# When the second half's operands are made, and on which engine the gate's minimum runs, in a hybrid decoder block

## The chip, the cores and the metric

The kernel runs on one core of a Trainium2 chip. Its engines are TensorE (PE in the profile, with its weight loads as PEld), VectorE (DVE), ScalarE (ACT) and GpSimd (POOL); SyncE (SP) issues the DMA transfers. Each engine runs its own queue strictly in order and waits on semaphores for the others. The metric is the time of one execution on the device in microseconds; the runs of the kernel before have a median of 2060.56 us.

## The reference

One decoder layer over 2048 positions of width 1024. The parts that matter here:

```python
h = rmsnorm(x, norm1_g[l])
proj = h @ w_in[l]
p_q, p_k, p_v, p_g, p_a, c_b, c_c, c_h = jnp.split(proj, splits, axis=-1)
gate_logits = (p_a @ w_gate_up[l] + b_gate[l]).astype(jnp.float32)
log_a = (jax.nn.log_sigmoid(gate_logits) / GATE_NORMALIZER)
o = gla_chunked(q, k, v, log_a)
o = rmsnorm(o, gla_norm_g[l])
o = o * jax.nn.silu(p_g)
u = c_c * c_h
o_conv = c_b * causal_depthwise_conv(u, conv_w[l])
x = x + jnp.concatenate([o_gla, o_conv], axis=-1) @ w_out[l]
h2 = rmsnorm(x, norm2_g[l])
x = x + (silu(h2 @ w_ffn_gate[l]) * (h2 @ w_ffn_up[l])) @ w_ffn_down[l]
return rmsnorm(x, norm_f_g)
```

## The kernel before

The 2048 positions are cut into four blocks of 512, and two blocks make a half. The input projection, then the output projection, then the feed-forward part run half by half. Everything is kept transposed: a tile has 128 features on the partitions and 512 positions.

**Products.** A float32 operand is split into a high and a low part of a shorter type (`split`, L162: a copy on ScalarE, L163, makes the high part, a subtraction on VectorE, L164, the low part). A product is then three matmuls: high x high, high x low, low x high (`product_step`, L443, lines 448 to 450). Over these, a Strassen scheme with seven products instead of eight combines four quarters of the weights with four quarters of the operands (`unit`, L452). The right-hand operands have seven kinds, B11, T1, T2, B21, T3, B22 and T4, each with four tiles; T1 to T4 are differences of quarters. The weights of a unit come as A11, S1, S2, A12, S3, S4, A22; they are split just ahead of their product into four buffers `wq`, so a split can be at most three products ahead. A product has 12 matmuls, a unit seven products. In a unit, c11 is copied out of the bank of the first product (`copied`, L476, copy on L480) before the third product S2 adds into the same bank; the later sums are made on VectorE (`plus`, L472, L473).

**The input projection** (`in_proj`, L749) has twelve units in each half: u = 0 to 3 make keys, queries and values, u = 4 and 5 the output gate (`silu`, L509, L512 on ScalarE), u = 6 to 11 the short convolution. The operands of the first half are made at the start (`build_first`). Those of the second half, x scaled by the norm's factors, are made in the background of the first half: `h1_ahead` (L646) calls `combine` (L278). That loads a quarter of x (`fetch`), scales it on VectorE (`quad`, `scaled`, L615), makes the differences on GpSimd and hands each operand to `put`. `put` stores three kinds whole (T3, B22 and T4, named in `WHOLE`) as float32. It splits the other four and stores high and low parts. Between the halves `load_pairs` (L662) loads them: a kind stored in two parts by one transfer, a kind stored whole by `load_whole`, which splits it after loading. An operand's tile can be loaded once the last product of the first half with its predecessor is done, since there are 28 operand tiles (`opp`).

**The gate.** `gate` (L691) multiplies the operands with the low-rank weights (32 matmuls into `a_ps`, L702), copies and splits the result (`a_sb`), and makes four products z (L724), each followed by `forget_gate` (L730). With s = z + b that computes log sigmoid(s) = min(s, 0) - ln(1 + exp(-|s|)): Abs, Exp and Ln on ScalarE (L733, L735, L736), the minimum and the subtraction on VectorE (L734, L737), then four scans over 128 positions and two small Exp on ScalarE (`em`, `el`).

**The recurrence.** `gla_half` (L801) goes over eight chunks of 128 positions in a half. Each chunk loads 14 small tiles, and has Exp, Ln and Square on ScalarE and small matmuls on TensorE.

**Order.** Background work is a list of generators. After each product `tick` (L241) counts `pace` and runs one step of the first generator at each second tick, or at each tick while `hurry` is set. The list of the first half holds the gate of the first half, row statistics, then `unhurried`, then `h1_ahead`; `gla_half(0)` is appended after the Silu units, and `gate(1)` when the second half begins. This sets the order in which the instructions are written. From it a scheduler fixes the order on each engine when the program is built, with its own estimate of when each instruction is ready. `tc.issue_after` (in `behind`, L155) asks that an instruction be queued after another one on the same engine; it adds no wait for another engine. The loads of ScalarE's function tables are put in afterwards, before each function that is not in the table set then resident.

Of the kernel before, what the change touches and what calls it, by code (L numbers as in the profile page):

```python
# [10 lines left out]
F32 = mybir.dt.float32  # L11
# [3 lines left out]
AF = mybir.ActivationFunctionType  # L15
ALU = mybir.AluOpType
# [3 lines left out]
P = 128  # L20
D = 1024
SEQ = 2048
PB = 512
# [21 lines left out]
WHOLE = ("T3", "B22", "T4")  # L45


C_G1, C_G2, C_GF, C_BG, C_GN, C_CW = 0, 8, 16, 24, 26, 27
N_SMALL = 39

# [2 lines left out]
def tile_hymba_block(ctx, tc, x, xt, win, wa, wgu, wout, wffn, wdown, wdown_first, small, out):  # L53
    nc = tc.nc
    act, dve, pool, pe = nc.scalar, nc.vector, nc.gpsimd, nc.tensor

    def pool_of(name, bufs, **kw):
        return ctx.enter_context(tc.tile_pool(name=name, bufs=bufs, **kw))

    const = pool_of("const", 1)  # L60
# [6 lines left out]
    dram = pool_of("dram", 1, space=DRAM)  # L67
# [19 lines left out]
    dve.memset(eps[:], EPS)  # L87
    sml = const.tile([P, N_SMALL], F32, name="sml")
    nc.sync.dma_start(sml[:], small)
    wgu_sb = mixer.tile([96, 256], F32R, name="wgu_sb")  # L90
    wa_sb = mixer.tile([P, 23 * 32], F32R, name="wa_sb")
    dve.memset(wa_sb[:].bitcast(F32), 0.0)
# [10 lines left out]
            [dram.tile([P, PB], F32, name=f"{name}{b}_{i}") for i in range(n)] for b in range(NB)  # L103
        ]

    def made_ahead(name, n):
        return dram.tile([P, PB] if n in WHOLE else [P, 2, PB], F32, name=name)

    s_kq, s_d, s_v, s_g = scratch("sk", 4), scratch("sd", 2), scratch("sv", 4), scratch("sg", 4)
    s_x1 = scratch("sx", KD)  # L110
# [15 lines left out]
        n: [made_ahead(f"sh{n}_{k}", n) for k in range(4)] for _, n in PRODUCTS  # L126
    }
    s_h1 = {
        n: [made_ahead(f"si{n}_{k}", n) for k in range(4)] for _, n in PRODUCTS
    }  # L130

    def col(c):
        return sml[:, c : c + 1]
# [7 lines left out]
    def bt(name, shape=(P, PB)):  # L141
        return bx[0].tile(list(shape), F32, name=name, tag="b")

    def load(dst, src):
        return nc.sync.dma_start(dst, src)

    def store(dst, src):
        return nc.sync.dma_start(dst, src)

    last_hi, last_lo, raw_loads = [], [], []  # L150
    last_out = []
    second_weights, unit_splits, unsplit = [], [], []

    @contextmanager
    def behind(marks):  # L155

        with ExitStack() as stack:
            for m in marks:
                stack.enter_context(tc.issue_after(m.ins))
            yield  # L160

    def split(src, hi, lo):  # L162
        last_hi[:] = [act.activation(hi, src, AF.Copy)]  # L163
        last_lo[:] = [dve.tensor_tensor(lo, src, hi.bitcast(F32), ALU.subtract)]  # L164
        return last_lo[0]
# [62 lines left out]


    background = []  # L230
    pace, ahead, hurry = [0], [], []

    def step():
        while background:
            try:
                next(background[0])
                return
            except StopIteration:
                background.pop(0)

    def tick():  # L241
        pace[0] += 1
        if pace[0] % 2 == 0 or hurry:
            step()
        elif ahead and pace[0] % 4 == 1:
            next(ahead[0], None)

# [8 lines left out]

    def unhurried():
        hurry.clear()
        yield

    def pause(n):
        for _ in range(n):
            yield
# [14 lines left out]
    def combine(src, g, rb, put):  # L278


        order = [kj for k in range(4) for kj in ((k, 0), (k, 1), (k + 4, 1), (k + 4, 0))]
        ahead = deque()

        def fetch():
            if order:
                k, j = order.pop(0)
                h = bt("h")
                load(h[:], src(k, j))
                ahead.append((k, j, h))

        def quad():
            k, j, h = ahead.popleft()
            fetch()
            return scaled(col(g + k), rb[j], h)

        fetch()
        fetch()
        for k in range(4):
            b11 = quad()
            put("B11", k, b11)  # L300
            yield
            b12, t1 = quad(), bt("t1")
            pool.tensor_tensor(t1[:], b12[:], b11[:], ALU.subtract)
            put("T1", k, t1)
            yield
            b22 = quad()
            pool.tensor_tensor(t1[:], b22[:], t1[:], ALU.subtract)
            put("T2", k, t1)
            yield
            pool.tensor_tensor(b12[:], b22[:], b12[:], ALU.subtract)  # L310
            put("T3", k, b12)
            yield
            b21 = quad()
            put("B21", k, b21)
            yield
            pool.tensor_tensor(t1[:], b21[:], t1[:], ALU.subtract)
            put("T4", k, t1)
            yield
            put("B22", k, b22)
            yield  # L320

    def build_first(quad, w):

# [128 lines left out]
    def unit(src, ops, into=None, onto=None, raw=None):  # L452

        w = unit_weights(src, raw)
        unit_splits[:] = last_hi + last_lo
        with behind(unit_splits):
            for y, o in unsplit:
                split(y[:], o[:, 0, :], o[:, 1, :])  # L460
        unsplit.clear()

        def mul(i, o=None):
            first = o is None
            o = bank() if first else o
            n, m = PRODUCTS[i]
            for k in range(len(ops[m])):
                product_step(o, w[n], ops[m], k, first)
            tick()
            return o  # L470

        def plus(t, o):  # L472
            dve.tensor_tensor(t[:], o[:], t[:], ALU.add)  # L473
            return t

        def copied(name, o, at):  # L476
            if onto is not None:
                return plus(onto[at], o)
            t = tt(name) if into is None else into[at]
            last_out[:] = [act.activation(t[:], o[:], AF.Copy)]  # L480
# [132 lines left out]
    def scaled(g, rb, h, into=None):  # L613
        y = h if into is None else into
        last_scaled[:] = [dve.scalar_tensor_tensor(y[:], h[:], g, rb[:], ALU.mult, ALU.mult)]  # L615
        return y
# [29 lines left out]
    def h1_ahead():  # L646

        def put(n, k, h):
            if n in WHOLE:
                store(s_h1[n][k][:], h[:])  # L650
                return
            hi, lo = [bx[0].tile([P, PB], F32R, name=e, tag="b") for e in ("hi", "lo")]
            split(h[:], hi[:], lo[:])
            for e, y in enumerate((hi, lo)):
                store(s_h1[n][k][:, e, :], y[:].bitcast(F32))

        for b in (2, 3):
            rbs[b] = rows_rstd(squares[b][:, :, 0], tables=False)
            yield
        yield from combine(lambda k, j: xt[2 + j, :, k, :], C_G1, (rbs[2], rbs[3]), put)  # L660

    def load_pairs(src):  # L662
        ops = no_operands()
        for _, n in PRODUCTS:
            ops[n] = [(load_whole if n in WHOLE else load_pair)(p) for p in src[n]]
        return ops

    def load_whole(src):
# [61 lines left out]
    def forget_gate(b, i, z, em, dn, el):  # L730
        bg = col(C_BG + i)
        t1, t2 = bt("g1"), bt("g2")
        act.activation(t1[:], z[:], AF.Abs, bias=bg)  # L733
        dve.tensor_scalar(t2[:], z[:], bg, 0.0, ALU.add, ALU.min)  # L734
        act.activation(t1[:], t1[:], AF.Exp, scale=-1.0)  # L735
        act.activation(t1[:], t1[:], AF.Ln, bias=one_t)  # L736
# [515 lines left out]
    for i in range(6):  # L1252
        load(carry[16 * i : 16 * i + 16, 0:2, :], wgu[0:16, :].rearrange("p (h c) -> p h c", c=P))
    ops, first, differences = build_h()
# [10 lines left out]
    ops = load_pairs(s_h1)  # L1265
# [122 lines left out]
```

## Time and profile before

| | |
|---|---|
| median of 3 runs | 2060.56 us (2059.81 to 2061.47) |
| span of the profiled execution | 2059.3 us |
| TensorE busy | 2018.4 us, 98% |
| VectorE, ScalarE, GpSimd busy | 1425.3, 959.7, 859.8 us |
| mean granted clock of TensorE | 0.996 |

In the profile's rows, a group is given by line, engine, operation, and output<-input by the program's names, with the count; then its busy time, the mean duration of one in ns, and the idle time of the engine before it. A row of waits reads "who <- for whom: us in total, times, longest". A row of the chain or of the timeline has start and duration in us. A row of windows has the length of the window and then pairs of busy time and count for PE, PEld, DVE, ACT and POOL, the granted clock, the share of DMA and GB/s. Matmuls overlap, so the time of one is read from the starts of two. SPq rows are the issues of DMA transfers.

### The profile page before, as it was taken

The numbers are of one execution on the slowest core, as the hardware profiler recorded it, in microseconds if no ns is written. First come the engines' busy times: TensorE is split into PE (matmuls) and PEld (weight loads), VectorE is DVE, ScalarE is ACT, GpSimd is POOL, SyncE is SP. The second block draws the span as 40 slices with busy tenths as digits, with TensorE's granted clock in tenths as the row PEclk, the third lists the DMA queues.
The fourth block names the chain that finished last, engine by engine and source line by source line (L and its number), as shares of the span: only waits on it lengthen the run. The fifth ranks groups of instructions, "written<-read, shape, count | busy, mean of one in ns | idle before, by whom it ended". The sixth has DMA issues, their size and how long they took to land.

```text
span 2059.3 us, 27063 instructions
## 1 busy us (share of the span) xinstructions
PE 2018.4 (98%) x9229; PEld 1657.3 (80%) x9229; DVE 1425.3 (69%) x2128; ACT 959.7 (47%) x1918; POOL 859.8 (42%) x622
## 2 busy tenths in 40 slices
PE   7999999999999999999999999999999999999997
PEld 6877888787888888888888878787888888878786
DVE  8789686559743886676675676767666666667774
ACT  6655365765542344444444452334434444453344
POOL 0345322122102564464564345534644544435544
PEclk9999999999999999999999999999999999999998
DMA  6378485416586873545454676476444434586653
GB/s 229 116 274 278 159 319 165 143 67 194 190 296 246 311 254 130 198 181 207 156 185 143 241 264 254 185 282 257 163 164 167 175 140 169 179 309 223 234 217 126
DMA packets 188729, 421.47 MB, mean 205 GB/s; under 512 B 19792, under 2 KB 65072, under 8 KB 178992
## 3 DMA queue, kind: packets, MB, share of 16 engines
q1 hardware_dynamic: 188592, 419.76, 57.2%
q8 instruction: 72, 1.18, 0.2%
q14 instruction: 65, 0.53, 0.1%
HBM read 274.98 MB, written 144.70 MB: 204 GB/s over the span
## 4 chain that ended last, share of the span: by engine, by line
PE 84%; DVE 7%; DMA 4%; ACT 3%; issue 1%; POOL 1%; SPq 0%; DVEq 0%; ACTq 0%; POOLq 0%
PE mm L448 24%; PE mm L449 23%; PE mm L450 23%; PE mm L945 3%; PE mm L948 3%; PE mm L946 3%; DVE wq L164 2%; DVE op L164 1%; DMA op<-sa_B 1%; DMA op<-sa_T 1%; PE a_ps L702 1%; ACT wq L163 1%; DMA siT<-lo 1%; PE o_ps L869 1%; PE o_ps L871 1%
## 5 line engine op out<-in xcount | busy, mean ns | idle before, releaser
L448 PE MATMUL mm<-op,wq 128*128 128x512 f32 x2499 | 973.7, 392 | 10.3 <-ACT c L480 5.3
L449 PE MATMUL mm<-op,wq 128*128 128x512 f32 x2499 | 972.5, 390 | 1.6 <-DVE op L164 1.6
L450 PE MATMUL mm<-op,wq 128*128 128x512 f32 x2499 | 961.3, 390 | 2.6 <-DVE wq L164 2.3
L164 DVE TENSOR_TENSOR wq<-raw,wq 128x512 fp32r<-128x512 f32 (+2 forms) x626 | 508.9, 818 | 262.6 <-ACT wq L163 260.0
L163 ACT ACTIVATE wq<-raw 128x512 fp32r<-128x512 f32 (+2 forms) x626 | 364.9, 589 | 585.6 <-PE mm L450 447.9
L448 PEld LDWEIGHTS mm<-op,wq 128*128 128x128 f32 x2499 | 468.9, 188 | 114.9 <-ACT c L480 8.0
L450 PEld LDWEIGHTS mm<-op,wq 128*128 128x128 f32 x2499 | 469.1, 188 | 103.8 <-DVE wq L164 6.1
L449 PEld LDWEIGHTS mm<-op,wq 128*128 128x128 f32 x2499 | 469.3, 188 | 99.1 <-DVE op L164 3.7
L432 POOL TENSOR_TENSOR raw<-s,raw 128x512 f32<-128x512 f32 (+2 forms) x97 | 133.3, 1374 | 518.5 <-DVE wq L164 474.7
L430 POOL TENSOR_TENSOR s<-raw 128x512 f32<-128x512 f32 (+2 forms) x97 | 127.4, 1313 | 247.5 <-DMA raw<-in_wffn_dram 90.7
L473 DVE TENSOR_TENSOR c<-mm,c 128x512 f32<-128x512 f32 x198 | 135.8, 686 | 72.7 <-PE mm L450 70.9
L473 DVE TENSOR_TENSOR y<-mm,y 128x512 f32<-128x512 f32 x185 | 126.9, 687 | 83.3 <-PE mm L450 82.9
L437 POOL TENSOR_TENSOR raw<-raw 128x512 f32<-128x512 f32 (+2 forms) x97 | 120.6, 1244 | 126.7 <-DVE wq L164 126.7
L927 POOL TENSOR_TENSOR ssx<-ssx,q 128x512 f32<-128x512 f32 x52 | 77.4, 1504 | 158.8 <-ACT q L926 158.5
L431 POOL TENSOR_TENSOR raw<-raw 128x512 f32<-128x512 f32 (+2 forms) x97 | 137.3, 1416 | 4.9
L480 ACT ACTIVATE c<-mm 128x512 f32<-128x512 f32 x198 | 116.1, 587 | 11.1 <-PE mm L450 9.3
L945 PE MATMUL mm<-op,wq 128*128 128x512 f32 x256 | 100.9, 395 | 0.0
L946 PE MATMUL mm<-op,wq 128*128 128x512 f32 x256 | 99.7, 389 | 0.0
L163 ACT ACTIVATE wq<-s 128x512 fp32r<-128x512 f32 (+2 forms) x97 | 56.9, 587 | 89.3 <-PE mm L450 85.4
L164 DVE TENSOR_TENSOR wq<-s,wq 128x512 fp32r<-128x512 f32 (+2 forms) x97 | 82.6, 852 | 2.8 <-ACT wq L163 2.1
L164 DVE TENSOR_TENSOR op<-op 128x512 fp32r<-128x512 f32 x94 | 76.8, 844 | 4.7 <-ACT op L163 4.6
L948 PE MATMUL mm<-op,wq 128*128 128x512 f32 x256 | 79.8, 390 | 0.0
(204 smaller groups left out, 1807.6 us busy)
## 6 DMA issues: line engine op xcount, KB each, us to landing
raw<-in_wffn_dram SPq DMA_DIRECT2D x44, 1024.0 KB, 6.5
sa_B<-so SPq DMA_DIRECT2D x47, 512.0 KB, 4.2
op<-sa_B SPq DMA_DIRECT2D x47, 512.0 KB, 7.1
raw<-in_win_dram SPq DMA_DIRECT2D x23, 1024.0 KB, 5.4
sa_T<-so SPq DMA_DIRECT2D x44, 512.0 KB, 4.5
op<-sa_T SPq DMA_DIRECT2D x44, 512.0 KB, 6.9
raw<-in_wdown_dram SPq DMA_DIRECT2D x24, 768.0 KB, 5.8
sx<-y SPq DMA_DIRECT2D x48, 256.0 KB, 4.0
```

Source lines behind the costliest of these rows:

```text
L163: last_hi[:] = [act.activation(hi, src, AF.Copy)]
L164: last_lo[:] = [dve.tensor_tensor(lo, src, hi.bitcast(F32), ALU.subtract)]
L430: pool.tensor_tensor(s1, a21, a22, ALU.add)
L431: pool.tensor_tensor(a21, a11, a21, ALU.subtract)
L432: pool.tensor_tensor(a11, s1, a11, ALU.subtract)
L448: pe.matmul(o[:], wh, xh, start=first and k == 0, stop=False, skip_group_check=True)
L449: pe.matmul(o[:], wh, xl, start=False, stop=False, skip_group_check=True)
L450: return pe.matmul(o[:], wl, xh, start=False, stop=k == n - 1, skip_group_check=True)
L473: dve.tensor_tensor(t[:], o[:], t[:], ALU.add)
L945: pe.matmul(o[e, j][:], wh, m[:, 0, :], start=k == 0, stop=False)
L946: pe.matmul(o[e, j][:], wh, m[:, 1, :], start=False, stop=False)
L948: pe.matmul(o[e, j][:], wl, ops[k][j][:, 0, :], start=False, stop=k == KD - 1)
```

## The change

Five things change.

1. T2 and B21 join the kinds of the second half that are stored whole (`WHOLE_H1`): `put` no longer splits them, and `load_pairs` splits them after loading.
2. In `combine`, when it is run for these operands (`with_marks`), the scalings are queued on VectorE behind the last sum (`last_plus`).
3. There, too, an operand's `put` comes one step later (`keep`, `kept`), with its instructions queued behind the last copy out of a bank and the last sum.
4. From the point `unhurried` on, and until the operands are done, `tick` runs a second step at each fourth tick (`steady`), so three steps in four ticks instead of two.
5. The gate's minimum moves: ScalarE makes Relu(-(z + b)), which is -min(z + b, 0), and VectorE's subtraction becomes one operation with the sign. For the bias a small tile `minus_bg` is made at the start.

```diff
+WHOLE_H1 = ("T2", "B21") + WHOLE
...
+    minus_bg = const.tile([P, 2], F32, name="minus_bg")
+    dve.tensor_scalar(minus_bg[:], sml[:, C_BG : C_BG + 2], -1.0, None, ALU.mult)
...
         if pace[0] % 2 == 0 or hurry:
             step()
+            if steady and pace[0] % 4 == 0:
+                step()
...
     def unhurried():
         hurry.clear()
+        steady.append(True)
         yield
+
+    def h1_paced():
+        with_marks.append(True)
+        yield from h1_ahead()
+        with_marks.clear()
+        steady.clear()
...
         def quad():
             k, j, h = ahead.popleft()
             fetch()
-            return scaled(col(g + k), rb[j], h)
+            with behind(last_plus if with_marks else []):
+                return scaled(col(g + k), rb[j], h)
+
+        def keep(*args):
+            made.append(args)
+            if not with_marks:
+                put(*made.popleft())
+
+        def kept():
+            while made:
+                with behind(last_out + last_plus):
+                    put(*made.popleft())
...
         for k in range(4):
+            kept()
             b11 = quad()
-            put("B11", k, b11)
+            keep("B11", k, b11)
             yield
...
         def plus(t, o):
-            dve.tensor_tensor(t[:], o[:], t[:], ALU.add)
+            last_plus[:] = [dve.tensor_tensor(t[:], o[:], t[:], ALU.add)]
             return t
...
-            if n in WHOLE:
+            if n in WHOLE_H1:
                 store(s_h1[n][k][:], h[:])
...
-            ops[n] = [(load_whole if n in WHOLE else load_pair)(p) for p in src[n]]
+            ops[n] = [(load_whole if n in WHOLE_H1 else load_pair)(p) for p in src[n]]
...
         act.activation(t1[:], z[:], AF.Abs, bias=bg)
-        dve.tensor_scalar(t2[:], z[:], bg, 0.0, ALU.add, ALU.min)
+        act.activation(t2[:], z[:], AF.Relu, bias=minus_bg[:, i : i + 1], scale=-1.0)
         act.activation(t1[:], t1[:], AF.Exp, scale=-1.0)
         act.activation(t1[:], t1[:], AF.Ln, bias=one_t)
-        dve.tensor_tensor(t2[:], t2[:], t1[:], ALU.subtract)
+        dve.scalar_tensor_tensor(t2[:], t2[:], -1.0, t1[:], ALU.mult, ALU.subtract)
...
-            h1_ahead(),
+            h1_paced(),
```

More of the change, by code (lines that the diff above doesn't have):

```diff
@@ L104, in scratch, with made_ahead @@
         ]
-    def made_ahead(name, n):
-        return dram.tile([P, PB] if n in WHOLE else [P, 2, PB], F32, name=name)
+    def made_ahead(name, n, whole=WHOLE):
+        return dram.tile([P, PB] if n in whole else [P, 2, PB], F32, name=name)
     s_kq, s_d, s_v, s_g = scratch("sk", 4), scratch("sd", 2), scratch("sv", 4), scratch("sg", 4)
@@ L128, in tile_hymba_block @@
     s_h1 = {
-        n: [made_ahead(f"si{n}_{k}", n) for k in range(4)] for _, n in PRODUCTS
+        n: [made_ahead(f"si{n}_{k}", n, WHOLE_H1) for k in range(4)] for _, n in PRODUCTS
     }
@@ L151, in tile_hymba_block @@
     last_out = []
-    second_weights, unit_splits, unsplit = [], [], []
+    second_weights, unit_splits, unsplit, last_plus, with_marks = [], [], [], [], []
     @contextmanager
@@ L230, in tile_hymba_block @@
     background = []
-    pace, ahead, hurry = [0], [], []
+    pace, ahead, hurry, steady = [0], [], [], []
     def step():
@@ L281, in combine @@
         order = [kj for k in range(4) for kj in ((k, 0), (k, 1), (k + 4, 1), (k + 4, 0))]
-        ahead = deque()
+        ahead, made = deque(), deque()
         def fetch():
@@ L298, in combine @@
         for k in range(4):
+            kept()
             b11 = quad()
-            put("B11", k, b11)
+            keep("B11", k, b11)
             yield
+            kept()
             b12, t1 = quad(), bt("t1")
             pool.tensor_tensor(t1[:], b12[:], b11[:], ALU.subtract)
-            put("T1", k, t1)
+            keep("T1", k, t1)
             yield
+            kept()
             b22 = quad()
             pool.tensor_tensor(t1[:], b22[:], t1[:], ALU.subtract)
-            put("T2", k, t1)
+            keep("T2", k, t1)
             yield
+            kept()
             pool.tensor_tensor(b12[:], b22[:], b12[:], ALU.subtract)
-            put("T3", k, b12)
+            keep("T3", k, b12)
             yield
+            kept()
             b21 = quad()
-            put("B21", k, b21)
+            keep("B21", k, b21)
             yield
+            kept()
             pool.tensor_tensor(t1[:], b21[:], t1[:], ALU.subtract)
-            put("T4", k, t1)
+            keep("T4", k, t1)
             yield
-            put("B22", k, b22)
+            kept()
+            keep("B22", k, b22)
             yield
+        kept()
     def build_first(quad, w):
```

## The prediction

> **What bounds the kernel now.** I read the page first, then who TensorE waits for, then ScalarE where those waits end. The page:
>
> ```profile
> span 2059.3 us, 27063 instructions
> PE 2018.4 (98%) x9229; PEld 1657.3 (80%) x9229; DVE 1425.3 (69%) x2128; ACT 959.7 (47%) x1918; POOL 859.8 (42%) x622
> ```
>
> TensorE is busy for 2018.4 of 2059.3 us, and the change leaves its instructions alone, so it can act only through TensorE's stops. The waits of TensorE between 86 and 240 us (the first half's projection, in which the second half's operands are made), then between 240 and 660 us (the second half's projection and the output projection):
>
> ```profile
> PE mm L450 <- DVE wq L164: 1.8, 4, 0.6
> PE mm L448 <- ACT c L480: 1.7, 1, 1.7
> ...
> PE sc L845 <- DVE kq L835: 1.3, 1, 1.3
> PE mm L448 <- DVE c L473: 0.9, 2, 0.7
> ```
>
> So 1.8 + 1.7 = 3.5 us is all that perfect operand making could win, and 2.2 us more lies in the later stretch. Before the first gate (86 us) and after the output projection (some 690 us) the changed program has the same order of work but for one small operation.
>
> What a late engine costs shows in the chain of waits that ends at 391.99 us:
>
> ```profile
> 382.60 1.28 ACT L512
> 383.90 0.63 ACT c L512
> ...
> 386.71 1.28 ACT L169
> ...
> 388.53 1.28 ACT L170
> ...
> 390.65 0.69 DVE osb L898
> 391.34 0.61 DVE c L473
> 391.99 0.50 PE mm L448
> ```
>
> The rows of 1.28 us are table loads. ScalarE switches between Silu (L512), Ln (L169) and Exp (L170) while the recurrence of the first half runs under the second half's Silu units, and TensorE stops behind it. The groups of ScalarE from 380 to 422 us count them:
>
> ```profile
> L512 ACT ACT_TABLE_LOAD x4 | 5.1, 1283 | 0.1
> ...
> L169 ACT ACT_TABLE_LOAD x2 | 2.6, 1283 | 0.0
> L170 ACT ACT_TABLE_LOAD x2 | 2.6, 1283 | 0.0
> ...
> L832 ACT ACT_TABLE_LOAD x1 | 1.3, 1283 | 0.6 <-issue 0.6
> L804 ACT ACT_TABLE_LOAD x1 | 1.3, 1283 | 0.0
> ```
>
> Ten loads of 1283 ns, and they cost TensorE about 0.7 us, because idle time lay between them. The gate of the second half comes later in this profile, from 445.89 us, when one table with Exp and Ln is resident; it needs no load.
>
> **The first half: operands.** Eight fewer splits (T2 and B21, four blocks each) leave ScalarE and VectorE, and 16 stores become 8. The waits of VectorE between 86 and 200 us, the chain there, and the windows of 50 us:
>
> ```profile
> DVE h L615 <- DMA h<-in_xt_dram: 6.1, 5, 1.9
> ...
> 150.10 7.62 DMA siT<-lo
> 157.77 0.73 issue
> 158.50 0.74 DVE h L615
> ...
> 100.00:150.00 50.00, 49.48 (x221) 40.26 (x220) 40.29 (x88) 31.58 (x67) 20.25 (x15) 1.00 0.73 251
> 150.00:200.00 50.00, 47.03 (x205) 37.93 (x204) 46.76 (x53) 23.59 (x46) 33.19 (x22) 1.00 0.87 304
> ```
>
> A scaling (L615) sits in VectorE's queue ahead of a weight's split, waiting for a load whose buffer waits for a store. VectorE (third pair) is busy 46.76 of 50 us in the second window. The marks only order instructions on one engine; they add no semaphore wait, and stores on SP keep their place. With the scaling behind a sum and eight splits gone I take 2.5 of the 3.5 us; bounds: a gain of 3.5, a loss of 1 if a queued load is met anyway. The new 128x2 negation runs while VectorE still waits for the first x: nothing, and at worst the 0.75 us of a full-width one.
>
> **The step from half to half.** T2 and B21 are now split after loading: 20 splits where there were 12. With the faster pace the recurrence also starts 96 matmuls sooner, so two more of its chunks fall into this stretch. From the first weight split of the second half's first unit to that of the next, I count on VectorE 38 full-width operations and 8 small ones in the changed order.
>
> ```profile
> 291.37 0.68 DVE L473 TENSOR_TENSOR c<-mm,c 128x512 f32<-128x512 f32 x1
> 291.97 0.68 DVE L164 TENSOR_TENSOR op<-op 128x512 fp32r<-128x512 f32 x1
> 292.57 0.69 DVE L164 TENSOR_TENSOR wq<-s,wq 128x512 fp32r<-128x512 f32 x1
> ...
> L164 DVE TENSOR_TENSOR op<-op 128x512 fp32r<-128x512 f32 x94 | 76.8, 844 | 4.7 <-ACT op L163 4.6
> ```
>
> One every 0.60 us at best makes 23 + 2.5 = 25.5 us, at 0.75 us (towards the group's mean of 844 ns) 31; TensorE needs 19.2 us for the unit (below) and 3 for a chunk. VectorE may be three products, 8.2 us, ahead. So it just holds, or fails by 1 to 3 us; I take 1, bounds 0 and 6 (twice the miss, for loads that come late). On SP the 28 small loads of those two chunks now stand among the operand loads:
>
> ```profile
> L148 SPq DMA_DIRECT2D siT<-hi x8: 319/350/607, 135.0 to 186.8; - x8
> ```
>
> At 0.35 us an issue (the median of the three) that is 9.8 us over two units, 38 us: hidden while the operand loads wait for their slots anyway, and part of the bound of 6 if not.
>
> **The gate on top of the Silu units.** The operand work now takes three steps in four ticks instead of two, 30 steps thus 40 ticks instead of 60. Everything queued behind it, the recurrence and then gate(1), comes 20 ticks or about three units sooner. In the changed program as built, the gate's 32 matmuls stand in the second Silu unit, 144 product matmuls earlier. ScalarE's order from there (a table load in brackets, S the sum weights):
>
> ```
> copy4(a_sb) split copy split copy | Abs Relu [.]Exp split [.]Ln
> Abs Relu [.]Silu [.]Exp em [.]Ln carry2 [.]el splitS1 splitS2
> Abs Relu em [.]Silu [.]Exp [.]Silu carry2 splitA12 [.]el [.]Ln
> Abs Relu [.]Silu splitS3 copy-c11 [.]Exp [.]em ee el splitS4 ...
> ```
>
> That is 18 loads over the two Silu units for 10 before, 14 of them behind the gate's matmuls, 12 of these before the copy of c11 of the next unit (u = 6). This copy decides: product S2 adds into the same bank, so TensorE can't start it before c11 is out. Prices, from TensorE and ScalarE in order of time:
>
> ```profile
> 445.69 0.40 PE L448 MATMUL mm<-op,wq 128*128 128x512 f32 x1
> 451.17 0.40 PE L724 MATMUL z<-a_sb,wgu_sb 96*128 96x512 f32 x1
> 451.41 0.40 PE L448 MATMUL mm<-op,wq 128*128 128x512 f32 x1
> ...
> 445.89 0.59 ACT L713 ACTIVATE a_sb<-a_ps 32x512 fp32r<-32x512 f32 x1 [6.74 <-PE a_ps L702]
> 449.03 0.60 ACT L505 ACTIVATE c<-mm 128x512 f32<-128x512 f32 x1
> 452.45 0.68 ACT L733 ACTIVATE g<-z,sml 128x512 f32<-128x512 f32 x1
> 453.16 0.64 ACT L735 ACTIVATE g<-g 128x512 f32<-128x512 f32 x1
> 453.82 0.73 ACT L736 ACTIVATE g<-g,ones 128x512 f32<-128x512 f32 x1
> 454.46 0.62 ACT L163 ACTIVATE wq<-raw 128x512 fp32r<-128x512 f32 x1
> 454.98 0.58 ACT L480 ACTIVATE c<-mm 128x512 f32<-128x512 f32 x1
> ...
> 87.70 0.75 DVE g L734
> ```
>
> Two products (24 matmuls) take 451.17 - 445.69 = 5.48 us, one 2.74, a unit of seven 19.2; a z matmul 0.24. TensorE's need, from the end of the gate's first matmuls: six products of this unit, three of the next (A11, S1, A12) and four small gate matmuls (z), 24.7 + 1.0 = 25.7 us.
>
> ScalarE has to do in that time: four part copies 3.1 (445.89 to 449.03, the wait for VectorE among them); 7 splits and 3 copies at about 0.52, 5.2; 4 Abs and 4 Relu at 0.63 (the Abs row's own 0.68, less overlap), 5.0; 3 Exp and 3 Ln at about 0.65, 3.9; 4 Silu at 0.6, 2.4; 4 carries and 4 small ones, 2.2 (estimated from their places in the same view); 12 loads at 1.30, 15.6. Sum 37.4, plus about 1 for the wait for a weight's slot: 38.4 us. TensorE stops for 38.4 - 25.7 = 12.7 us, in several pieces (S1, A12 and c11 are each late in turn). Two more loads with Exp, em, ee, el stand ahead of split S4: 4.5 us and 0.7 for VectorE's part, against 2.7 for S2's product, 2.4 more. Together 15.1 us. Without loads the same queue would end at 22.8 us, before it is needed. Against it stand the waits at L845 and L473 that this order replaces, 1.3 + 0.9 = 2.2. Net 12.9 us. Bounds: 9 (a third of the misses hidden by splits already done) and 20 (VectorE's waits for the gate added).
>
> The Relu for the minimum takes 0.75 us (L734) off VectorE and puts about 0.68 (as L733) on ScalarE, four times in each half. In the second half it is in the sum above. In the first, ScalarE (fourth pair of the windows above) is busy 31.58 of 50 us around the gate and has room, so I put nothing; without that room it is 4 x 0.68 = 2.7 us.
>
> The Trainium skill ("ScalarE: Activation LUTs", What ACT_TABLE_LOAD costs) states about 1283 ns for a load and as much again for the drain, 2.66 us a switch, and advises to group calls by table set. The trace agrees on 1283, and the next operation starts 1.30 us after the load did (382.60 to 383.90), so no further 1.38 us shows; by the Trainium skill's 2.66 the 14 loads would add 19 us to mine.
>
> **Sum.** 2059.3 - 2.5 + 1 + 12.9 = 2070.7 us of span. The median of the runs, 2060.56, lies 1.3 above the profiled span, so 2072.
>
> **Rivals.** (1) Faster: the loads fall into idle time, as ten of them nearly do now. For: 0.7 us for ten. Against: 37.4 us of work for 25.7, without a gap. It decides if the queue up to the copy of c11 ends within 25.7 us. Then the operands' 2.5 and the later 2.2 are won: 2060.56 - 4.7 = 2056. Chance 0.09.
>
> (2) VectorE becomes the bound at the step between halves: 844 ns throughout for 38 operations, 32 + 2.5 less 22.2 and half its lead, gives 6 to 8 us instead of 1: 2078. Chance 0.14.
>
> (3) A switch costs twice the 1.30 us where ScalarE's queue is full, the pipeline running empty before each: 14 loads, 18 us more: 2090. For it speaks only that such rows are few; against it that each of the rows above goes on after 1.30. Chance 0.04. (This is the rule of the Trainium skill above.)
>
> (4) The weights' lead of three products, 8.2 us, takes up part of the queue: 15.1 - 8.2 = 6.9 us stay, and 2060.56 + 6.9 - 2.2 - 2.5 + 1 = 2064, no change that can be told. For it: S1 and A12 are split ahead. Against it: c11 can't be copied ahead of its own products. Chance 0.08.
>
> **Numbers.** The forecast, 2072, has 0.65. Its own bounds give 2060.56 + (9 - 2.2 - 3.5) = 2064 and 2060.56 + (20 - 2.2 + 1 + 6) = 2085, all against it at once, so 2083 is enough; downwards it takes in (4) and 2 us below it, 2062. Left out are (1), (3) and the far ends of the rest. About 0.2% (4 us) is what this measurement can tell from no change: faster 0.07 (most of (1)), within 0.11 (the rest of it, (4) and a trace of the forecast's low end), slower 0.82.
>
> **What would show it.** Right: some 18 table loads in the two Silu units of the second half; TensorE waiting 12 to 18 us there, on ScalarE's copy L513 and on weight splits; its waits in 86 to 240 us near 1 us. Wrong: TensorE's waits after the gate under 6 us, or more than 4 us of them between the last unit of the first half and the second unit of the second. If the operands' waits stay at 3.5 us, the scalings were not their cause.

## The result, and the profile after

The changed kernel is slower: 2081.79 us median (2079.72 to 2083.92, 4 runs) beside 2061.01 us (2059.81 to 2065.28, 4 runs) for the kernel before on the same chip, a ratio of 1.0093, interval 1.008 to 1.0106. That is 20.8 us by the medians (16.5 to 21.8 by the interval) where 11.4 were forecast. The profiled execution has a span of 2082.2 us, 22.9 more than before's; it is the slowest of the four, 2.1 us over their median. Its page, with busy time and share by engine:

```profile
span 2082.2 us, 27076 instructions
PE 2027.2 (97%) x9229; PEld 1662.3 (80%) x9229; DVE 1421.4 (68%) x2121; ACT 973.7 (47%) x1934; POOL 865.9 (42%) x622
```

TensorE has the same 9229 matmuls but is busy for 8.8 us more (2027.2 against 2018.4). So 14.1 us of the 22.9 are stops, and 8.8 are matmuls that took longer. Line numbers are those of each kernel: in the kernel after, the product's matmuls are L481 to L483, the copy of c11 L513, the splits L168 and L169, Silu L545, the gate's Exp and Ln L768 and L769, and `el` L778; in the kernels of the experiments they lie some lines off. The stops, as the waits of TensorE in the kernel after, of 86 to 245, 245 to 370 and 370 to 470 us (who <- for whom: us in total, times, longest):

```profile
PE mm L481 <- ACT c L513: 3.4, 2, 3.1
...
PE mm L481 <- ACT c L513: 2.0, 1, 2.0
PE mm L481 <- ACT op L168: 1.6, 1, 1.6
PE mm L481 <- DVE c L506: 0.7, 1, 0.7
PE ot L938 <- DVE osb L931: 0.4, 1, 0.4
PE mm L482 <- DVE op L169: 0.3, 1, 0.3
...
PE mm L481 <- ACT wq L168: 5.2, 1, 5.2
PE mm L481 <- ACT c L513: 4.7, 2, 4.3
PE ot L938 <- DVE osb L931: 0.9, 1, 0.9
```

Before had 3.5, nothing and 0.7 us in these three stretches, and 2.1 us more at 472 to 600 us (the row of 1.3 in the prediction and two waits under half a microsecond); there, after has none. The operand stretch is thus no better, the step between the halves lost 5.0 us, and the second half's Silu units lost 10.8. The table loads in those units, alone, from the groups of ScalarE in 400 to 470 us:

```profile
L545 ACT ACT_TABLE_LOAD x6 | 7.7, 1283 | 0.1
L768 ACT ACT_TABLE_LOAD x4 | 5.1, 1283 | 0.1
L769 ACT ACT_TABLE_LOAD x3 | 3.8, 1283 | 0.1
L778 ACT ACT_TABLE_LOAD x2 | 2.6, 1283 | 0.0
L174 ACT ACT_TABLE_LOAD x1 | 1.3, 1283 | 0.0
L175 ACT ACT_TABLE_LOAD x1 | 1.3, 1283 | 0.0
L837 ACT ACT_TABLE_LOAD x1 | 1.3, 1283 | 0.0
```

These are 18, as forecast. ScalarE ahead of the longest stop, in order of time (start, duration, what; in brackets idle time and its releaser):

```profile
430.60 1.28 ACT L768 ACT_TABLE_LOAD   x1
431.89 0.63 ACT L768 ACTIVATE g<-g 128x512 f32<-128x512 f32 x1
432.43 0.61 ACT L168 ACTIVATE wq<-raw 128x512 fp32r<-128x512 f32 x1
433.06 1.28 ACT L769 ACT_TABLE_LOAD   x1
...
442.97 1.28 ACT L778 ACT_TABLE_LOAD   x1
444.27 0.21 ACT L778 ACTIVATE el<-g 128x4 f32<-128x4 f32 x1
444.38 0.61 ACT L168 ACTIVATE wq<-s 128x512 fp32r<-128x512 f32 x1
```

Between the weight split of 432.43 and the next, of S1, at 444.38 ScalarE is never idle, and TensorE stands still behind it. The Exp of 431.89 us and the Ln of 434.36 us each have a load ahead of them, while in the kernel before the gate's Exp and Ln follow each other (453.16 and 453.82 us) without one. A version in which one table serves both here was not tried. What happens next on TensorE was in no term of my sum:

```profile
439.25 0.39 PE L482 MATMUL mm<-op,wq 128*128 128x512 f32 x1
439.48 0.39 PE L483 MATMUL mm<-op,wq 128*128 128x512 f32 x1
445.05 0.80 PE L481 MATMUL mm<-op,wq 128*128 128x512 f32 x1 [5.18 <-ACT wq L168]
...
447.19 0.63 PE L482 MATMUL mm<-op,wq 128*128 128x512 f32 x1
447.61 0.63 PE L483 MATMUL mm<-op,wq 128*128 128x512 f32 x1
```

Ahead of the stop the matmuls start 0.23 us apart, behind it 0.42 to 0.43. Three windows of the kernel after show the granted clock (third figure from the end; of the pairs these rows have TensorE's alone) around the stop that ends at 219.81 us:

```profile
215.66:219.08 3.42, 1.08 (x5) 1.00 0.81 305
219.08:225.90 6.82, 6.09 (x14) 0.50 0.72 247
225.90:229.32 3.42, 3.42 (x16) 1.00 0.63 179
```

So the clock falls to half, here for 6.8 us. By the trace's records of the clock it is at half from 219.08 to 225.90, from 301.00 to 304.41, from 444.36 to 451.18 and from 461.42 to 464.84 us, at each of the four longest stops. Counted from the trace, 13 matmuls are slow behind the stop at 220 us, 6 behind that at 301 us, 12 behind that at 445 and 6 behind that at 462: 37, at 0.20 us each 7.4 us. The account of the span is then: operand stretch 3.4 - 3.5 + 2.6 (13 slow matmuls) = +2.5; step between the halves 5.0 + 1.2 = +6.2; gate 10.8 - 0.7 - 2.1 + 3.6 = +11.6. That is 20.3 of 22.9 us; the rest is not traced, but it lies ahead of 797 us: from there to the end the two kernels take the same time within 0.5 us.

### The profile page after: what moved, and what is told of

The parts are those of the page before. It is cut to its first block, busy times and chain, and to the rows that moved or that the text cites. A ratio compares the mean times of both kernels' runs of the same rounds, so it can differ in the third digit from the quotient of the medians.

```text
span 2082.2 us, 27076 instructions
## 1 busy us (share of the span) xinstructions
PE 2027.2 (97%) x9229; PEld 1662.3 (80%) x9229; DVE 1421.4 (68%) x2121; ACT 973.7 (47%) x1934; POOL 865.9 (42%) x622
## 4 chain that ended last, share of the span: by engine, by line
PE 84%; DVE 6%; ACT 4%; DMA 3%; issue 1%; POOL 1%; SPq 0%; DVEq 0%; ACTq 0%; POOLq 0%
PE mm L481 24%; PE mm L483 24%; PE mm L482 24%; PE mm L978 3%; PE mm L979 3%; PE mm L981 3%; DVE wq L169 2%; DVE op L169 1%; DMA op<-shT 1%; ACT wq L168 1%; PE a_ps L735 1%; PE o_ps L902 1%; ACT op L168 1%; PE o_ps L904 1%; DVE h L648 1%
## 5 line engine op out<-in xcount | busy, mean ns | idle before, releaser
L481 PE MATMUL mm<-op,wq 128*128 128x512 f32 x2499 | 979.1, 394 | 25.7 <-ACT c L513 14.5
L483 PE MATMUL mm<-op,wq 128*128 128x512 f32 x2499 | 964.2, 391 | 2.1 <-DVE wq L169 1.9
L169 DVE TENSOR_TENSOR wq<-raw,wq 128x512 fp32r<-128x512 f32 (+2 forms) x626 | 514.7, 827 | 292.8 <-ACT wq L168 290.8
L168 ACT ACTIVATE wq<-raw 128x512 fp32r<-128x512 f32 (+2 forms) x626 | 364.3, 588 | 611.8 <-PE mm L483 464.2
L481 PEld LDWEIGHTS mm<-op,wq 128*128 128x128 f32 x2499 | 470.9, 189 | 133.6 <-ACT c L513 18.3
L483 PEld LDWEIGHTS mm<-op,wq 128*128 128x128 f32 x2499 | 470.9, 188 | 105.0 <-DVE wq L169 5.8
L513 ACT ACTIVATE c<-mm 128x512 f32<-128x512 f32 x198 | 115.6, 586 | 14.0 <-PE mm L483 12.6
L168 ACT ACTIVATE wq<-s 128x512 fp32r<-128x512 f32 (+2 forms) x97 | 56.8, 585 | 90.8 <-PE mm L483 85.7
L169 DVE TENSOR_TENSOR op<-op 128x512 fp32r<-128x512 f32 x102 | 83.9, 851 | 5.2 <-ACT op L168 5.2
L169 DVE TENSOR_TENSOR wq<-s,wq 128x512 fp32r<-128x512 f32 (+2 forms) x97 | 82.0, 845 | 2.7 <-ACT wq L168 1.9
```

Of the source, the lines that this page charges most:

```text
L481: pe.matmul(o[:], wh, xh, start=first and k == 0, stop=False, skip_group_check=True)
L483: return pe.matmul(o[:], wl, xh, start=False, stop=k == n - 1, skip_group_check=True)
```

## The experiments

All ratios are to runs of the kernel before on the same chip, in the same series. Each diff is against the kernel that the text names.

### Is it the table loads? Is it the gate's place?

First the gate of the second half put later, the rest as after:

```diff
-    background.append(gate(1, ops))
+    background.extend([pause(6), gate(1, ops)])
```

> The kernel after with a pause of 6 steps (12 ticks) put ahead of the second half's gate, so that its first matmuls come again where they came before, behind the Silu units; 10 table loads in the built order instead of 23. Theory A (the gate in the Silu units costs 10.8 us of stops and 4.0 us of slow matmuls after them): all of that goes, the stops at 220 and at 290 to 313 us stay, time 2066 to 2069 us, and no stop over 2 us between 320 and 700 us. Rival (ScalarE's queue is too full whatever the order, and the stop only moves): 2076 us or more.

Measured: 2070.69 us (2068.84 to 2071.49), ratio 1.0036 [1.0023, 1.0049]. TensorE's waits of that kernel from 370 to 520 us:

```profile
PE sc L878 <- DVE kq L868: 1.4, 1, 1.4
PE mm L481 <- DVE c L506: 1.4, 1, 1.4
PE ot L938 <- DVE osb L931: 0.9, 1, 0.9
```

The stops of 5.2 and 4.3 us are gone, and the time falls by 11.1 us (2081.79 to 2070.69); 1.4 and 1.4 us of waits come at 480 to 485 us, some 9 us behind where the kernel before has its own. The time is 1.7 us above the top of my bracket.

Putting the gate later also moves its work on TensorE and VectorE. To take away the loads alone, the second half's Silu was replaced by a copy at the same place (this kernel leaves the function out, so it doesn't compute the layer):

```diff
-                store(s_g[2 * half + j][i0 + r][:], silu(c, p)[:])
+                store(s_g[2 * half + j][i0 + r][:], silu(c, p, AF.Copy if half else AF.Silu)[:])
```

> The kernel after with the second half's Silu left out: a plain copy stands in its place, of the same shape, at the same place in ScalarE's queue, so the order on ScalarE is that of after and only 17 of its 23 table loads are gone (the copy needs no table). The gate stays where after has it, in the Silu units. Theory (it is the table loads that make TensorE stop there): the stops at 445 and 462 us (5.2 + 4.3 us, 4.0 us of slow matmuls behind them) go, as the same queue without loads ends before it is needed; time 2066 to 2069 us, as with the gate put later. Rival (the gate's work itself is too much for ScalarE and VectorE in these units): 4 to 9 us of stops stay, time 2072 to 2078 us.

Measured: 2066.21 us (2063.57 to 2069.02), ratio 1.0023 [1.0014, 1.0033]. All of TensorE's waits from 370 to 470 us, and ScalarE at the place shown above:

```profile
PE o_ps L902 <- DVE scores L881: 1.2, 1, 1.2
```

```profile
427.87 0.64 ACT L768 ACTIVATE g<-g 128x512 f32<-128x512 f32 x1
428.63 0.63 ACT L168 ACTIVATE wq<-raw 128x512 fp32r<-128x512 f32 x1
429.17 0.71 ACT L769 ACTIVATE g<-g,ones 128x512 f32<-128x512 f32 x1
...
434.57 0.21 ACT L778 ACTIVATE el<-g 128x4 f32<-128x4 f32 x1
434.69 0.61 ACT L168 ACTIVATE wq<-s 128x512 fp32r<-128x512 f32 x1
```

The same queue, without loads, needs 6.1 us between the two splits instead of 12.0, and the stops are gone. The gate may stand where it stands: the loads are the cost, 2081.79 - 2066.21 = 15.6 us by the medians, slow matmuls included (before's medians in the two series are 2061.0 and 2061.1), or 14.4 by the two ratios.

### Does the pace bring the loss?

At first I held the faster pace to be the cause of everything. So it was taken away from after, and added alone to before:

```diff
-        steady.append(True)
```

> The kernel after with the old pace of the background (two steps in four ticks), all else as changed. As built, the gate of the second half and the recurrence stand again where they stood before. Theory A (the pace alone brings the loss, because it puts the gate into the Silu units, 10.8 us of stops and 4.0 us of half-rate matmuls after them, the recurrence into the step between the halves, 5.0 + 1.2 us, and the operands' last steps into the units at 200 to 245 us, 3.1 + 2.6 us): no stop of TensorE over 2 us between 86 and 700 us, the operands' gain of 3 us kept, time 2056 to 2061 us. Theory B (the marks or the kinds stored whole make the stops at 220 us and at 290 to 313 us by themselves): these stay, time 2066 to 2070 us.

> The kernel before with only the faster pace added; scalings, puts, kinds stored whole and the gate's minimum as before. Theory A (pace alone): the gate stands in the second Silu unit and the loss of 10.8 + 4.0 us behind it is all there, and a stop at the step from half to half; time 2075 to 2083 us. Theory B (the loss needs the changed operands or the Relu on ScalarE): under 2070 us. If only the stops at the step between the halves need the extra splits: 2061 + 14.8 = 2076 us with nothing at 290 to 313 us.

Measured: after without the pace 2083.06 us (2080.43 to 2085.18), ratio 1.0095 [1.008, 1.011]; before with the pace 2075.43 us (2072.44 to 2077.19), 1.0057 [1.0042, 1.0072]. The second shows the gate's stops (4.3 and 2.8 us at 437 and 452 us) as expected. The first refutes theory A: the gate is back at its old place, and the kernel is as slow as after. Theory B, that the marks or the kinds stored whole make stops by themselves, holds in kind, but its bracket is 13 us too low. The stops are elsewhere; the two longest rows from 245 to 320 us:

```profile
PE sc L877 <- DVE kq L867: 5.0, 1, 5.0
PE mm L480 <- DVE c L505: 3.6, 1, 3.6
```

The reason is in when the 16 scalings run. The groups of the scalings' line, of before, after, and after without the pace (count, shortest, median and longest in ns, then first and last start in us):

```profile
L615 DVE SCALAR_TENSOR_TENSOR h<-h,sml,rb_ps x16: 733/743/748, 129.3 to 184.4; 128x512 f32<-128x512 f32 x16
```

```profile
L648 DVE SCALAR_TENSOR_TENSOR h<-h,sml,rb_ps x16: 730/736/748, 126.5 to 220.5; 128x512 f32<-128x512 f32 x16
```

```profile
L647 DVE SCALAR_TENSOR_TENSOR h<-h,sml,rb_ps x16: 727/738/742, 125.6 to 263.9; 128x512 f32<-128x512 f32 x16
```

Before, the scheduler ran the scalings well ahead of the place where they are written. Tied to a sum, they come no earlier than that sum, and the last one 36 us later at the new pace, 80 us later at the old one. There they run into the convolution units and, at the old pace, into the loading of the second half's operands.

### The order of the operand work by itself

Theory C, that the marks hold the operands back, was tried both ways. After without `with_marks.append(True)`, and before with the marks and the later puts alone:

> The kernel after without the order of the operand work: scalings and puts are queued as the scheduler likes and puts aren't kept a step; faster pace, five kinds whole and Relu stay. Theory C (the marks hold the 16 scalings back: 129 to 184 us before, 126 to 220 after, 126 to 264 with the marks at the old pace; their late end meets VectorE's conv work and makes the stop at 220 us): the scalings end near 184 us, the stop at 220 us (3.1 + 2.6 us) goes, a stop near 160 us like that of before and of the pace alone comes back (1.7 to 4 us), the gate's 14.8 us stay; time 2077 to 2081 us. Rival (the stop at 220 us comes from the faster recurrence or the splits): it stays and the time is 2082 us or more.

> The kernel before with only the order of the operand work added (scalings behind the last sum, puts one step later behind the last copy and sum); old pace, three kinds whole, minimum on VectorE. Theory C (the marks alone hold the operands back, past the end of the first half): scalings to about 264 us, stops of 10 us or more at 260 to 310 us, no stop over 2 us in 86 to 245 us; time 2074 to 2085 us. Rival (the two extra kinds stored whole made the stops of that stretch): under 2068 us.

Measured: without the marks 2083.33 us (2079.17 to 2084.04), ratio 1.0092 [1.0075, 1.0109]; marks alone 2080.63 us (2079.06 to 2082.34), 1.0086 [1.0071, 1.0101]. The marks alone end the scalings at 264.1 us and bring waits of which these are the longest from 245 to 320 us, while from 86 to 245 us only 0.5 and 0.2 us are left:

```profile
PE sc L877 <- DVE kq L867: 9.5, 1, 9.5
PE mm L480 <- DVE c L505: 4.2, 1, 4.2
```

That is theory C. Without them the scalings end at 178.0 us and the stop at 220 us is gone, again as it says. But the time didn't fall under after's: waits of 2.1 and 1.5 us come back between 86 and 205 us, the gate's stops stay at 5.2 and 4.3 us, and between 86 and 2000 us the clock is at half for 23.9 us instead of 20.5. The median is 2.3 us over the top of my bracket. So at the faster pace the marks neither win nor lose anything that the time shows; alone they cost some 18 us.

### The kinds stored whole, the Relu, the recurrence

Five kinds whole and the Relu on the kernel before; the Relu alone; and after with the first half's recurrence (and so the gate) put back to its old place:

```diff
-        background.append(gla_half(half))
+        background.extend([pause(0 if half else 10), gla_half(half)])
```

> The kernel before with the two kinds more stored whole and the Relu on ScalarE, at the old pace and without the order of the operand work. Theory C: eight splits and eight stores less up to 190 us take 1 to 2.5 us off the stops of the operand stretch, 8 more splits between the halves find room (VectorE had no late split there before), gate and recurrence stay; time 2058 to 2063 us, the same as before or a little faster. Rival (the extra splits alone overload VectorE between the halves, as my bound of 6 us has it): 2064 to 2067 us, with stops on op splits at 285 to 310 us.

> The kernel before with the gate's minimum on ScalarE alone. My sum put nothing for it in the first half, and with the gate at its old place nothing else. Theory (four times 0.68 us more in ScalarE's queue and a longer chain to the scans put the gate's VectorE work into the next units): the waits at 470 to 505 us grow from 1.6 us (0.28 + 1.29) to about 4 us (the 1.56 + 1.33 + 1.15 us seen with the Relu and the kinds stored whole); time 2 to 3 us over before. Rival (that growth came with the kinds stored whole): within 1 us of before.

> The kernel after with a pause of 10 steps (20 ticks) put ahead of the first half's recurrence, and so of the gate behind it; the operands are still made at the faster pace. Theory A (two more chunks of the recurrence in the step between the halves make the stops at 290 to 313 us, 5.0 + 1.2 us, and the gate in the Silu units those after 440 us, 14.8 us): both go, the stop at 220 us (3.1 + 2.6 us) stays, time 2060 to 2064 us. Rival (eight more operand splits between the halves are enough for the stops at 290 to 313 us): 2066 to 2069 us with those stops still there.

Measured: whole and Relu 2066.43 us (2064.56 to 2068.56), ratio 1.0019 [1.001, 1.0029]; Relu alone 2062.42 us (2060.1 to 2064.18), 1.0006 [0.9996, 1.0015]; recurrence later 2070.59 us (2066.61 to 2072.77), 1.004 [1.0027, 1.0052]. TensorE's only wait of 245 to 370 us, with five kinds and the Relu on before, then with the recurrence later:

```profile
PE mm L479 <- DVE c L504: 2.3, 1, 2.3
```

```profile
PE mm L481 <- DVE c L506: 2.3, 1, 2.3
```

Where the recurrence stands at its old place, five kinds whole cost one stop of 2.3 us, with 7 slow matmuls (1.4 us) behind it. It falls on a sum, not on the operand splits as my rival had it: VectorE is busy with splits of operands and weights while TensorE needs its sum. The pace alone, with three kinds and the recurrence early, has 2.4 us of stops at 293 to 304 us and no slow matmul there. After has both causes and 6.2 us in all. With five kinds and the Relu the time is over theory C's bracket and inside the rival's. With the recurrence later it is over both: its profile, of the fastest of the six runs, has the forecast stops gone and this one left, but the median is 4 us over that run, and the profile can't show where those go. The Relu alone has waits of 4.0 us at 465 to 505 us where before has 1.6; the time says at most 0.15% (3 us), and can't be told from no change.

### Is there a better version?

Without the two kinds and the Relu, and with recurrence and gate at their old places, only the marks are left, at two paces (for the second, `steady` runs a step at every tick and the pause is 15):

> The kernel before with the order of the operand work, three steps in four ticks as in the kernel after, and a pause of 10 steps ahead of the first half's recurrence, so that recurrence and gate stand where they stood before; three kinds whole, minimum on VectorE. So this is the kernel after without its later recurrence and gate, its kinds stored whole and its Relu. Theory C: the stop at 220 us (2.8 to 3.3 us and 7 to 13 slow matmuls) is all that is left, the stretch between the halves has no stop over 1 us; time 2061 to 2065 us. Rival (the stop at 295 us belongs to the late operands, not to the splits of T2 and B21): it stays, 2.3 us and 1.4 of slow matmuls, 2065 to 2068 us.

> The kernel before with the order of the operand work (marks, puts a step later), a step at every tick while it lasts, and a pause of 15 steps ahead of the first half's recurrence, so that recurrence and gate stand where they stood before; three kinds whole, minimum on VectorE. Theory C (the marks are worth 3 us up to 205 us, and cost only where the operands end late): the 16 scalings end before 200 us, no stop over 1.7 us from 86 to 320 us, time 2058 to 2062 us, the same as before or up to 4 us under it. Rival (the marks put the scalings into VectorE's full stretches whatever the pace): a stop of 2 to 4 us near 180 to 220 us, time 2064 to 2068 us.

Measured: three of four 2062.78 us (2060.13 to 2066.58), ratio 1.0008 [0.9999, 1.0018]; every tick 2067.27 us (2066.85 to 2069.5), 1.0031 [1.0019, 1.0043]. The first has no wait at all from 245 to 370 us, so the stops there do belong to the extra splits and the early recurrence. At 216 and 221 us it has stops of 2.0 and 2.1 us, shorter than forecast and with no slow matmul behind them. The windows of 86 to 205 and 205 to 245 us of that kernel:

```profile
86.00:205.00 119.00, 118.53 (x526) 97.36 (x525) 99.03 (x164) 69.62 (x141) 51.83 (x36) 1.00 0.63 217
205.00:245.00 40.00, 35.94 (x157) 29.11 (x156) 30.17 (x42) 17.40 (x34) 17.89 (x13) 1.00 0.74 241
```

Before, TensorE is busy for 115.47 and 40.00 us there. The marks win 3.1 us and give back 4.1. At every tick the late end is at 205 us and the gain is gone too (stops of 2.5 us at 197 and 1.6 us at 228 us). None of the twelve kernels beats before.

### How long must a stop be to lower the clock?

On the kernel before, the copy of c11 made several times over in chosen feed-forward units:

```diff
+        for _ in range(COPIES.get(unit_count[0], 1) - 1):
+            act.activation(c11[:], oa[:], AF.Copy)
+        unit_count[0] += 1
```

> The kernel before, with the copy of c11 out of its bank made 6, 7, 8, 9, 10, 11, 12, 14, 16, 20 and 24 times over in every second unit of the first feed-forward half (same values, the bank is only let go later). This makes TensorE's stops there graded, from under 1 us to some 10 us. Theory (a stop of about 1.8 us or more lowers the granted clock for a while after it, matmuls then come at 0.43 us instead of 0.23): after stops under 1.7 us no slow matmul, after each over 2 us 6 to 13 of them, that is 1.2 to 2.8 us more per stop, whatever the stop's length; the mean granted clock falls. Rival (the slow matmuls belong to the place, not to the stop): matmuls at 0.23 us behind all of these stops. Time: 2061 us plus the stops (sum some 35 us) plus 8 x 2 us by the theory, plus the stops alone by the rival.

Measured: 2099.06 us (one run). The stops didn't grow with the number of copies, since the weights' splits between them came late too and cut each into several; the longest is 2.6 us. Three windows, each behind one stop, of 2.64, 2.13 and 1.52 us:

```profile
1074.90:1079.00 4.10, 4.05 (x11) 0.58 0.66 240
1215.30:1219.40 4.10, 3.46 (x13) 1.00 0.00 0
1121.30:1126.00 4.70, 4.64 (x12) 0.67 0.49 195
```

So length alone doesn't decide: 2.13 us cost nothing, 1.52 us lowered the clock. In all fourteen profiles, counted from the traces behind 86 us, two of 96 stops of 1.2 to 1.75 us had slow matmuls behind them. Of 29 stops of 1.77 to 9.5 us, 25 had, 4 to 13 of them each, and the longest stops don't have the most. The other four are 1.98 to 2.13 us long.

The traces' records of the clock say more. In each of the fourteen, the clock changes only at instants that lie a multiple of 3.41 us apart, and so the half rate lasts 3.41, 6.83 or 10.24 us. I cut the traces at these instants into steps of 3.41 us and added up TensorE's idle time in each, from 60 to 1990 us. In 23 steps at full clock it is idle for over 1.95 us, as in the first window shown above for the kernel after (3.42 - 1.08 = 2.34 us), and the clock is halved at the end of each of them. It is never halved at the end of a step with under 1.49 us idle. Of the 33 steps in between, five end in half rate. So what counts is the idle time that falls into one step. The four long stops without slow matmuls leave at most 1.94 us in one, since an edge cuts them. Between 1.5 and 1.95 us it stays open, and there the stops of 1.52 and 2.13 us fall too (1.52 and 1.88 us in one step). This was read off the traces afterwards; no run was made to test it.

## Why the prediction was right, and where it wasn't

- **The time: inside the range, by its width.** 2081.8 us is 9.8 over the forecast of 2072 and 1.2 under the top, 2083. The three terms of the sum, -2.5 + 1 + 12.9 = 11.4, measure 2.5 + 6.2 + 11.6 = 20.3; only the third was near. Of its signs of being right the 18 loads came; the 12 to 18 us of waits on copy and splits were 9.9, and the waits of 86 to 240 us were 3.4 and not near 1.
- **Direction and main cause: right.** The gate on top of the Silu units makes 18 table loads, and without loads the time is 14.4 to 15.6 us less; the sum had 15.1 before what it replaces. The parts inside differ. I had 12.7 us of stops up to the copy of c11 and 2.4 more ahead of split S4; the waits are 5.2 + 4.3 = 9.5 us up to the copy and 0.4 after it, with 0.9 of another kind, and 3.6 us of half-rate matmuls, which I didn't know of, make up for it. The 2.2 us that the order replaces were won. Net 11.6 in the profile for 12.9: that it came so near is partly luck.
- **Operands in the first half: -2.5 forecast, +2.5 measured, outside its bounds (-3.5 to +1).** The step that failed is "The marks only order instructions on one engine; they add no semaphore wait, and stores on SP keep their place". As to what a mark adds, no run speaks against it. I didn't ask what it takes away: the scheduler's freedom to run the scalings early, which before used. The stops up to 205 us went, as I had reckoned (TensorE busy 118.55 us for 115.47), and one of 3.1 us with 13 slow matmuls came at 220. It was the marks that took the old ones away: marks alone leave 0.7 us of waits in 86 to 245 us, five kinds whole without marks 2.7 of the 3.5. My sign, waits that stay at 3.5 us clear the scalings, would have misled, as the sum is the same (3.4) and the waits are others. ScalarE there:

```profile
218.64 0.63 ACT L168 ACTIVATE hi<-c 128x512 fp32r<-128x512 f32 x1 [2.20 <-DVE c L826]
219.18 1.06 ACT L513 ACTIVATE c<-mm 128x512 f32<-128x512 f32 x2
```

  The copy that TensorE waits for (L513) stands behind a split that waits 2.20 us for VectorE (L826), which is then splitting a late operand and weights. The last scalings and their splits fall among the convolution's VectorE work.
- **From half to half: +1 forecast, bounds 0 and 6; 6.2 measured.** The right mechanism, mis-sized, and by the prediction's own mark (over 4 us there) wrong. I counted 38 operations on VectorE against the time that TensorE needs and found them to fit; the stops come from the order, an operand's split ahead of a sum or a copy, and from the clock. The extra splits are worth 3.7 us (2.3 + 1.4) without the earlier recurrence, and the earlier recurrence 2.4 us without them. Rival (2), 6 to 8 us for this step, was nearest.
- **The clock: not in the sum.** Its mean of 0.996 stood in my table, and I priced each stop at its own length. The 37 slow matmuls cost 7.4 us, a third of the loss. The Trainium skill ("TensorE: Matmul & The Clock Gate", HAM oscillation) gives about 3.4 us of idle time as the gap from which the clock is halved; here stops of 1.8 to 3.1 us did it as well, so by its figure alone the two stops of under 3.4 us in the kernel after (301 and 220 us), with 19 slow matmuls, would have cost nothing more.
- **Relu and minus_bg at nothing:** no more than 3 us on before.
- **The other rivals.** (1) fell: 18 loads didn't fit in idle time. (3) fell: after each load the next operation starts 1.29 to 1.30 us later (430.60 to 431.89), in a full queue too, and without the five loads between the two splits the queue is 5.9 us shorter (12.0 to 6.1), 1.2 us a load. So the further 1.38 us of drain that the Trainium skill ("ScalarE: Activation LUTs", What ACT_TABLE_LOAD costs) gives isn't seen here either. (4) fell: the first split behind the loads was itself the late one.
- **The faster pace makes up for the marks' late end**, and I read the pace only by its side effects. Marks alone 2080.6, pace alone 2075.4, both with recurrence and gate put back 2062.8 us: the pace cures most of what the marks do, and its own price is that everything queued behind it comes too early.

## What to carry to other kernels

An order that is forced on an engine takes away what the scheduler did on its own: look up when the tied instructions ran before, and when they can run at the earliest now. A faster background pace moves everything that is queued behind it; ask which of its functions will then alternate with which table, and put a pause there if they clash. Price a stop of TensorE of 2 us or more at its length plus 1 to 3 us: in these profiles 25 of the 29 stops of 1.77 us and more had slow matmuls behind them.

## What wasn't expected of the hardware

After 25 of 29 stops of 1.77 us and more the granted clock is 0.5 for one to three steps of 3.41 us, and a matmul of 512 columns comes each 0.43 us instead of 0.23. The steps lie on a fixed grid in each trace, and 1.95 us of idle time within one was always enough. In the kernel before the longest stop between 86 us and the end is 1.74 us, and no matmul is slow behind it.
